# Average pooling over one axis: the last row's store moved from inside a hand-synchronised section to behind it

## The chip, the cores and the metric

One core of one Trainium2 chip. The metric is the device time of one execution in microseconds (us), median of several runs; lower is better. The profile is one execution taken by the hardware profiler; its span is about 1.8 us shorter than the timed value of the same execution (1553.8 against 1555.6 for the kernel before). Every run in this document is of the fast state, with a granted clock of 1.0; the kernel does not use the TensorE at all.

## The reference

`x` is 64 x 256 x 8192 in float32; each group of four neighbours along the last axis is averaged.

```python
def reference(x, kernel_size, stride):          # both 4
    ...
    for i in range(out_len):                    # out_len = 2048
        start = i * stride
        output[:, :, i] = np.mean(x[:, :, start : start + kernel_size], axis=2)
    return output
```

That is 536.87 MB to read, 134.22 MB to write, and three additions and one multiplication per output.

## The kernel before

The 16384 rows are cut into 64 tiles of 128 partitions x 2 rows: 8.39 MB in, 2.10 MB out each. SP (SyncE) issues the loads into two input buffers, VectorE adds pairs twice, ScalarE multiplies by 1/4 in place and issues the store. There are four output buffers. All of this stands in a critical section: a stretch in which the author places every wait by hand and the framework (the layer that otherwise places waits) puts in none. Only the end matters here. `E` is 15, so `E * U + 3` is the last tile. It is loaded, summed and stored in two single rows.

```python
        def store(eng, h, u, r0=0, r1=R, again=False):
            eng.wait_ge(s_act, h * U + (u + 1 + (r1 - 1 if r1 - r0 < R else 0)))
            eng.dma_start(
                out=og[:, h * U + u, r0 * OL : r1 * OL], in_=obuf(u, r0, r1)
            ).then_inc(s_out[u] if again else s_fin, 16)
...
        # SP's stream, behind all loads:
        for u in range(1, U - 1):
            store(nc.sync, E, u)                 # tiles 1 and 2 of the last four
        store(nc.sync, E, U - 1, R - 1, R)       # last row of the last tile
...
        # ScalarE's stream at the end:
        scale(E, 1)
        scale(E, 2)
        scale(E, 3, 0, 1)
        store(nc.scalar, E, 3, 0, 1)             # first row of the last tile
        scale(E, 3, 1, 2)

    with tc.tile_critical():                     # a second section
        nc.sync.wait_ge(s_out[0], E * 16 + 16)
        nc.sync.wait_ge(s_fin, 64)               # the four late stores have landed
```

"Ring" in this document means the queue that one issuing engine feeds: SP's is q1 in the profile, ScalarE's is q10.

Of the kernel before, what the change touches and what calls it, by code (L numbers as in the profile page):

```python
# [1 line left out]

# [4 lines left out]



_R = 2  # L10

_NIN = 2
_NOUT = 4


@with_exitstack
def kernel(
    ctx: ExitStack,
    tc: tile.TileContext,
    x: bass.AP,  # L20
    kernel_size: bass.AP,
    stride: bass.AP,
    out: bass.AP,
):
    nc = tc.nc
    K = int(kernel_size)
    assert K == int(stride) == 4
    P = nc.NUM_PARTITIONS
    dt = x.dtype
    inv_k = 1.0 / float(K)  # L30

    xf = x.flatten_outer_dims()
    of = out.flatten_outer_dims()
    rows, L = xf.shape
    OL = of.shape[1]
    R = _R
    T, OT = R * L, R * OL
    assert OL * K == L and rows % (P * R * _NOUT) == 0
    NT = rows // (P * R)

    xg = xf.rearrange("(t p r) m -> p t (r m)", p=P, r=R)
    og = of.rearrange("(t p r) m -> p t (r m)", p=P, r=R)

    pool = ctx.enter_context(tc.tile_pool(name="buf", bufs=1))
    xin = pool.tile([P, _NIN * T], dt)
    res = pool.tile([P, _NOUT * OT], dt)



    s_in = [tc.alloc_semaphore(f"s_in{b}") for b in range(_NIN)]  # L50
    s_out = [tc.alloc_semaphore(f"s_out{b}") for b in range(_NOUT)]
    s_dve = tc.alloc_semaphore("s_dve")
    s_act = tc.alloc_semaphore("s_act")
    s_half = tc.alloc_semaphore("s_half")
    s_last = tc.alloc_semaphore("s_last")
    s_fin = tc.alloc_semaphore("s_fin")

    with tc.tile_critical():  # L58



        U = _NOUT
        E = NT // U - 1

        def load(h, u, r0=0, r1=R, wait=True):
            b = u % _NIN
            if wait:
                nc.sync.wait_ge(s_dve, h * U + (u - _NIN + 1))
            nc.sync.dma_start(  # L69
                out=xin[:, b * T + r0 * L : b * T + r1 * L],  # L70
                in_=xg[:, h * U + u, r0 * L : r1 * L],
            ).then_inc(s_last if r0 > 0 else s_in[b], 16)

        def obuf(u, r0=0, r1=R):
            return res[:, u * OT + r0 * OL : u * OT + r1 * OL]

        def store(eng, h, u, r0=0, r1=R, again=False):
            eng.wait_ge(s_act, h * U + (u + 1 + (r1 - 1 if r1 - r0 < R else 0)))
            eng.dma_start(
                out=og[:, h * U + u, r0 * OL : r1 * OL], in_=obuf(u, r0, r1)  # L80
            ).then_inc(s_out[u] if again else s_fin, 16)

        def pairs(out, src):
            v = src.rearrange("p (m k) -> p m k", k=2)
            return nc.vector.tensor_tensor(  # L85
                out=out, in0=v[:, :, 0], in1=v[:, :, 1], op=mybir.AluOpType.add
            )

        def add_up(h, u, r0=0, r1=R):

            b = u % _NIN
            if r0 > 0:
                nc.vector.wait_ge(s_last, 16)
            else:
                nc.vector.wait_ge(s_out[u], h * 16)
                nc.vector.wait_ge(s_in[b], h * (U // _NIN * 16) + (u // _NIN + 1) * 16)  # L96
            src = xin[:, b * T + r0 * L : b * T + r1 * L]
            half = src[:, : (r1 - r0) * L // 2]
            pairs(half, src).then_inc(s_half, 1)
            nc.vector.wait_ge(s_half, h * U + (u + 1 + (r0 > 0)))  # L100
            pairs(obuf(u, r0, r1), half).then_inc(s_dve, 1)

        def scale(h, u, r0=0, r1=R):
            nc.scalar.wait_ge(s_dve, h * U + (u + 1 + (r0 > 0)))
            o = obuf(u, r0, r1)
            nc.scalar.mul(o, o, inv_k).then_inc(s_act, 1)  # L106



        for u in range(_NIN):  # L110
            load(0, u, wait=False)
        with nc.sync.Fori(0, E) as h:
            for u in range(_NIN, U + _NIN):
                load(h, u)
        for u in range(_NIN, U - 1):
            load(E, u)
        for r in range(R):
            load(E, U - 1, r, r + 1, wait=r == 0)
        for u in range(1, U - 1):
            store(nc.sync, E, u)  # L120
        store(nc.sync, E, U - 1, R - 1, R)


        with nc.vector.Fori(0, E) as h:
            for u in range(U):
                add_up(h, u)
        for u in range(U - 1):
            add_up(E, u)
        for r in range(R):
            add_up(E, U - 1, r, r + 1)  # L130



        scale(0, 0)
        nc.scalar.wait_ge(s_dve, 2)
        store(nc.scalar, 0, 0, again=True)
        with nc.scalar.Fori(0, E) as h:
            for u in range(1, U + 1):
                v = u % U
                nc.scalar.wait_ge(s_dve, h * U + (u + 1))  # L140
                nc.scalar.mul(obuf(v), obuf(v), inv_k).then_inc(s_act, 1)  # L141
                nc.scalar.wait_ge(s_act, h * U + (u + 1))
                nc.scalar.dma_start(out=og[:, h * U + u, :], in_=obuf(v)).then_inc(
                    s_out[v], 16
                )
        scale(E, 1)
        scale(E, 2)
        scale(E, 3, 0, 1)
        store(nc.scalar, E, 3, 0, 1)
        scale(E, 3, 1, 2)  # L150


    with tc.tile_critical():
        nc.sync.wait_ge(s_out[0], E * 16 + 16)
        nc.sync.wait_ge(s_fin, 64)


# [1 line left out]
_INS = ['x', 'kernel_size', 'stride']  # L159
_OUTS = [((64, 256, 2048), 'float32')]  # L160

_NUMBERS = {'kernel_size': 4, 'stride': 4}


# [26 lines left out]
```

## Time and profile before

| | before |
|---|---|
| time, median of 3 (range) | 1555.30 us (1555.29 to 1555.41) |
| span of the profile | 1553.8 us |
| data moved, mean rate | 671.10 MB, 432 GB/s |
| VectorE, ScalarE busy | 54%, 15% |
| one period of two tiles in mid-run | 48.36 us |

The page of the kernel before, its span, the DMA row (busy tenths in 40 equal slices) and the chain that ended last:

```profile
span 1553.8 us, 982 instructions
...
DMA  9999999999999999999999999999999999999999
...
HBM read 536.87 MB, written 134.22 MB: 432 GB/s over the span
...
DMA 72%; DVE 27%; issue 0%; SPq 0%; ACT 0%; DVEq 0%
```

The 16 DMA engines are at least nine tenths busy in every slice. The chain names VectorE (DVE) for 27%, but while it sums, stores still stand in the rings. Two tiles (20.97 MB) take 48.36 us, which is 433.6 GB/s. The Trainium skill, "DMA: Bandwidth & Descriptors", section "Specifications", gives 435 GB/s as the ceiling of the fabric; the mid-run rate of this trace agrees with that to within half a per cent. So only the first and the last few microseconds can give anything.

The timeline of the kernel before at its end (start, duration, engine, line, operation; in brackets the idle time of the engine before it and what ended it; SPq is SP's own sequence of instructions):

```profile
1537.92 4.42 DVE L85 TENSOR_TENSOR xin<-xin 128x4096 f32<-128x4096 f32 x1 [2.84 <-DMA xin<-in_x_dram]
1542.38 2.29 DVE L85 TENSOR_TENSOR res<-xin 128x2048 f32<-128x2048 f32 x1
1544.71 1.91 ACT L106 ACTIVATE res<-res 128x2048 f32<-128x2048 f32 x1 [7.68 <-DVE res L85]
1546.64 0.33 SPq L79 DMA_DIRECT2D out_dram<-res  x1
```

The last load has landed at 1537.9, the last scaling ends at 1546.62, and the last store is issued 0.02 us later. The DMA issues on the page (KB each, median us from issue to landing) and the windows at the end (the last two numbers are DMA share and GB/s; a packet counts wholly in the window in which it starts, so a share can lie above 1):

```profile
out_dram<-res SPq DMA_DIRECT2D x2, 2048.0 KB, 27.1
out_dram<-res ACTq DMA_DIRECT2D x1, 1024.0 KB, 13.0
out_dram<-res SPq DMA_DIRECT2D x1, 1024.0 KB, 5.9
```

```profile
1547.00:1549.00 2.00, 0.00 (x0) 0.00 (x0) 0.00 (x0) 1.00 0.99 422
1549.00:1551.00 2.00, 0.00 (x0) 0.00 (x0) 0.00 (x0) 1.00 0.99 418
1551.00:1553.00 2.00, 0.00 (x0) 0.00 (x0) 0.00 (x0) 1.00 0.27 115
```

The last megabyte lands 5.9 us after its issue because older stores are still ahead of it; the engines stay full until about 1551. Finally SP's own instructions behind that landing, those of the framework's end of program (L186), then those of the second section (L153); the three numbers are shortest, median and longest duration in ns, then first and last start:

```profile
L186 SPq EVENT_SEMAPHORE  x5: 17/17/5077, 1547.4 to 1553.7; - x5
L186 SPq DRAIN  x3: 7/7/7, 1553.0 to 1553.3; - x3
L186 SPq COMPARE_BRANCH  x1: 38/38/38, 1552.7 to 1552.7; - x1
```

```profile
L153 SPq NOP  x2: 13/13/13, 1547.4 to 1553.0; - x2
L153 SPq EVENT_SEMAPHORE  x1: 17/17/17, 1552.8 to 1552.8; - x1
L153 SPq DRAIN  x1: 7/7/7, 1552.9 to 1552.9; - x1
```

SP waits 5.08 us for the last landing, until about 1552.6. Then come a branch (1552.7), a semaphore (1552.8), a drain (1552.9) and a no-operation (1553.0), which leave the section, and only then the drains and barriers of the end of the program (1553.0 to 1553.8). (The wait and the branch belong to the section, though the records put them under L186.)

### The profile page before, as it was taken

How to read it: one execution, taken by the hardware profiler on the slowest of the kernel's cores; microseconds unless marked ns; L12 is line 12 of the kernel's file. 1: busy time of each engine (PE TensorE's matmuls, PEld its weight loads, DVE VectorE, ACT ScalarE, POOL GpSimd, SP SyncE). 2: the span in 40 equal slices, each digit the busy share in tenths (PEclk: the TensorE clock that was granted, in tenths of full speed). 3: DMA queues.
4: the chain of work that ended last, by engine and by line, in shares of the span. 5: the costliest groups of instructions: out<-in, count | busy, mean ns of one | idle time of the engine just before them, and what ended most of it. 6: DMA issues, size and time to landing. Idle time of an engine off the chain costs nothing.

```text
span 1553.8 us, 982 instructions
## 1 busy us (share of the span) xinstructions
DVE 839.8 (54%) x130; ACT 232.9 (15%) x66; POOL 0.2 (0%) x4
## 2 busy tenths in 40 slices
DVE  3645546456464564654646546455464554645546
ACT  1111011110111101101011010110111101111011
POOL 0000000000000000000000000000000000000000
DMA  9999999999999999999999999999999999999999
GB/s 405 423 434 439 439 439 434 417 443 427 439 439 437 434 417 434 438 439 432 442 427 426 433 434 444 439 434 423 429 435 439 439 439 434 415 436 436 439 425 405
DMA packets 18721, 671.10 MB, mean 432 GB/s; under 512 B 2081, under 2 KB 2081, under 8 KB 2081
## 3 DMA queue, kind: packets, MB, share of 16 engines
q1 hardware_dynamic: 9792, 542.12, 80.6%
q10 hardware_dynamic: 8928, 128.98, 19.4%
q14 instruction: 1, 0.00, 0.0%
HBM read 536.87 MB, written 134.22 MB: 432 GB/s over the span
## 4 chain that ended last, share of the span: by engine, by line
DMA 72%; DVE 27%; issue 0%; SPq 0%; ACT 0%; DVEq 0%
DMA xin<-in_x_dram 72%; DVE xin L85 18%; DVE res L85 9%; SPq L69 0%; ACT res L106 0%; DVEq L96 0%; SPq L186 0%; SPq L58 0%
## 5 line engine op out<-in xcount | busy, mean ns | idle before, releaser
L85 DVE TENSOR_TENSOR xin<-xin 128x8192 f32<-128x8192 f32 (+1 forms) x65 | 556.4, 8561 | 702.7 <-DMA xin<-in_x_dram 702.7
L141 ACT ACTIVATE res<-res 128x4096 f32<-128x4096 f32 x60 | 217.0, 3616 | 1226.0 <-DVE res L85 1226.0
L85 DVE TENSOR_TENSOR res<-xin 128x4096 f32<-128x4096 f32 (+1 forms) x65 | 283.3, 4359 | 2.2
L106 ACT ACTIVATE res<-res 128x4096 f32<-128x4096 f32 (+1 forms) x5 | 14.7, 2933 | 86.8 <-DVE res L85 86.8
L106 ACT ACT_TABLE_LOAD x1 | 1.3, 1283 | 0.9 <-SPq L58 0.9
L172 POOL MEMSET const-bfloat16-1.0<- 128x1 bf16 x1 | 0.1, 102 | 0.0
L172 POOL MEMSET const-uint8-127<- 128x1 uint8 x1 | 0.1, 101 | 0.0
L172 POOL MEMSET const-float32-0.0<- 128x1 f32 x1 | 0.1, 99 | 0.2 <-issue 0.2
L172 POOL MEMSET const-float32-1.0<- 128x1 f32 x1 | 0.1, 98 | 0.0
## 6 DMA issues: line engine op xcount, KB each, us to landing
out_dram<-res ACTq DMA_DIRECT2D x61, 2048.0 KB, 52.4
xin<-in_x_dram SPq DMA_DIRECT2D x2, 4096.0 KB, 29.5
out_dram<-res SPq DMA_DIRECT2D x2, 2048.0 KB, 27.1
out_dram<-res ACTq DMA_DIRECT2D x1, 1024.0 KB, 13.0
out_dram<-res SPq DMA_DIRECT2D x1, 1024.0 KB, 5.9
xin<-in_x_dram SPq DMA_DIRECT2D x63, 34.9
```

The costliest lines, as they stand in the source:

```text
L85: return nc.vector.tensor_tensor(out=out, in0=v[:, :, 0], in1=v[:, :, 1], op=mybir.AluOpType.add)
L106: nc.scalar.mul(o, o, inv_k).then_inc(s_act, 1)
L141: nc.scalar.mul(obuf(v), obuf(v), inv_k).then_inc(s_act, 1)
L172: nc = _bacc.Bacc("TRN2", target_bir_lowering=False, num_devices=1)
```

## The change

The intent: take the last store and the waits for the late stores out of the hand-synchronised sections, so that one section is left and it does not stay open for the late stores. The last store now stands behind the section, where the framework places the wait for it. That store stands in SP's ring behind the other late ones.

```diff
-        store(nc.sync, E, U - 1, R - 1, R)
+        store(nc.sync, E, U - 1, R - 1)          # now the first row, on SP
...
         scale(E, 3, 0, 1)
-        store(nc.scalar, E, 3, 0, 1)
         scale(E, 3, 1, 2)
 
-    with tc.tile_critical():
         nc.sync.wait_ge(s_out[0], E * 16 + 16)   # now the end of the first section
-        nc.sync.wait_ge(s_fin, 64)
+
+    nc.sync.dma_start(
+        out=og[:, NT - 1, (R - 1) * OL :], in_=res[:, _NOUT * OT - OL :]
+    )
```

(The semaphore `s_fin` goes, and the helper `store` loses two arguments.)

More of the change, by code (lines that the diff above doesn't have):

```diff
@@ L55 @@
     s_last = tc.alloc_semaphore("s_last")
-    s_fin = tc.alloc_semaphore("s_fin")
     with tc.tile_critical():
@@ L75, in obuf, with store @@
             return res[:, u * OT + r0 * OL : u * OT + r1 * OL]
-        def store(eng, h, u, r0=0, r1=R, again=False):
-            eng.wait_ge(s_act, h * U + (u + 1 + (r1 - 1 if r1 - r0 < R else 0)))
+        def store(eng, h, u, r1=R):
+            eng.wait_ge(s_act, h * U + (u + (1 if r1 == R else r1)))
             eng.dma_start(
-                out=og[:, h * U + u, r0 * OL : r1 * OL], in_=obuf(u, r0, r1)
-            ).then_inc(s_out[u] if again else s_fin, 16)
+                out=og[:, h * U + u, : r1 * OL], in_=obuf(u, 0, r1)
+            ).then_inc(s_out[u], 16)
         def pairs(out, src):
@@ L135 @@
         nc.scalar.wait_ge(s_dve, 2)
-        store(nc.scalar, 0, 0, again=True)
+        store(nc.scalar, 0, 0)
         with nc.scalar.Fori(0, E) as h:
```

## The prediction

> **What bounds the kernel.** The DMA engines. The profile page shows them busy 9 tenths or more in all 40 slices, moving 671.10 MB at 432 GB/s over the 1553.8 us span. VectorE is busy 54%, ScalarE 15%. The chain of waits is 72% loads landing and 27% VectorE sums, but the queues hold stores while the sums run. So only fewer bytes, or less idle time of the 16 engines at the start or end, can shorten it. The change touches only the end.
>
> **The end now**, from the timeline and the issue records:
> - last load landed about 1537.9; the last sums and the scaling end at 1546.62;
> - last-row store (1 MB) issued on SP at 1546.64, about 5.9 us to landing (1552.55);
> - the Scalar queue's store of the row before: issued 1537.05, landed about 1550.4;
> - between 1546.6 and the end 2.07 MB still move, so about 1.0 MB of older stores stand ahead of the last 1 MB. The DMA share by stretch is 0.99 from 1547 to 1551 and 0.27 from 1551 to 1553.
> - SP's wait in the second critical section is 5.08 us (1547.5 to 1552.6); branch at 1552.7, drains and barriers 1553.0 to 1553.8.
>
> So the tail is a drain of bytes.
>
> **What the change does.** Same bytes, same 16 engines.
> 1. The next-to-last row's store moves from the Scalar ring to the SP ring, behind tile 2's store. Order only: both rings feed the same engines (the Trainium skill, "DMA: Bandwidth & Descriptors", section "Issuing engines are not separate DMA queues"; this trace agrees: 434 GB/s with both rings at 1540 to 1542, 431 with SP's almost alone at 1537 to 1540). Worth 0, at most +/-0.3 us.
> 2. The last store leaves the section, so it is issued after the section's exit instead of after the scaling semaphore. Now Scalar and Vector drain at 1547.1 and 1547.2 and SP passes at 1547.4 to 1547.5. So I expect its issue at about 1547.4 to 1547.7 instead of 1546.64: +0.8 to +1.1 us. A DMA needs about 1 us from issue to first byte (the first load: issued 0.95, first packets between 1.5 and 2.5), so its bytes could start at about 1548.5. The older stores keep the engines busy until about 1549.0 (1.0 MB at 430 GB/s = 2.4 us, an estimate). So most of the delay is hidden; engines that drain early may idle some tenths: +0 to +0.6 us.
> 3. The second section goes: SP's wait chain and branch between landing (1552.55) and the drains (1553.0) is about 0.4 us. The framework's own wait for its store replaces it: -0.3 to 0 us.
> 4. The other stores land before the last one, so no longer waiting for them gains nothing.
>
> **On the critical path:** about -0.3 to +0.6 us in 1555, under 0.05%.
>
> **Prediction:** 1555.4 us, range 1554.6 to 1556.3. Chances: faster by over 2%: 0.003; within 2%: 0.994; slower by over 2%: 0.003.
>
> **What would show each step:** (1) in the windows after 1538, still 420 to 440 GB/s, and no store issue on the Scalar queue after 1483; (2) SP's last store issue at 1547.4 to 1547.7 with landing after about 5 us rather than 5.9, and DMA share about 0.95 or more from 1547 to 1551; (3) the gap from last landing to the end of the span 1.0 to 1.3 us; everything before 1530 identical within 0.1 us.
>
> **What would make it wrong:** if section exit makes SP wait for older stores to land (then the last 1 MB runs alone: about +3 us) or if a single ring drains more slowly than two.

## The result, and the profile after

| | before | after |
|---|---|---|
| time, median (range) | 1555.36 us (1555.29 to 1555.46, 4 runs) | 1554.80 us (1554.77 to 1555.00, 4 runs) |
| ratio, 95% interval | | 0.9997, 0.9979 to 1.0014 |
| span of the profile | 1553.8 us | 1553.0 us |

A ratio is the mean time of one kernel's fast runs over that of the other's of the same rounds, so it is not quite the ratio of the medians in the table. The interval contains 1. A difference of 0.56 us in 1555 is thus not settled by this ratio; what follows rests on the traces.

The timeline of the kernel after at its end, then its issues and its windows:

```profile
1537.54 4.42 DVE L85 TENSOR_TENSOR xin<-xin 128x4096 f32<-128x4096 f32 x1 [2.86 <-DMA xin<-in_x_dram]
1541.99 2.29 DVE L85 TENSOR_TENSOR res<-xin 128x2048 f32<-128x2048 f32 x1
1544.32 1.91 ACT L106 ACTIVATE res<-res 128x2048 f32<-128x2048 f32 x1 [7.70 <-DVE res L85]
1546.36 0.33 SPq L155 DMA_DIRECT2D out_dram<-res  x1
```

```profile
out_dram<-res SPq DMA_DIRECT2D x2, 2048.0 KB, 26.1
out_dram<-res SPq DMA_DIRECT2D x2, 1024.0 KB, 9.4
```

```profile
1547.00:1549.00 2.00, 0.00 (x0) 0.00 (x0) 0.00 (x0) 1.00 1.02 430
1549.00:1551.00 2.00, 0.00 (x0) 0.00 (x0) 0.00 (x0) 1.00 1.01 426
1551.00:1553.00 2.00, 0.00 (x0) 0.00 (x0) 0.00 (x0) 1.00 0.17 70
```

Two things are to be seen. The last sums already begin 0.38 us earlier than before (1537.54 against 1537.92), in a part of the program that the change does not touch. And the store is issued 0.13 us after the last scaling (1546.23) instead of 0.02 us, so leaving the section delayed it by 0.11 us only. Why so little is shown by SP's instructions of the section's exit (L57) and by what SP waited for:

```profile
L57 SPq NOP  x2: 13/13/13, 0.7 to 1546.3; - x2
L57 SPq EVENT_SEMAPHORE  x2: 17/3512/7007, 1537.2 to 1537.4; - x2
L57 SPq COMPARE_BRANCH  x1: 38/38/38, 1537.0 to 1537.0; - x1
L57 SPq DRAIN  x1: 7/7/7, 1537.3 to 1537.3; - x1
```

```profile
SPq L57 <- DVEq L57: 7.0, 1, 7.0
...
SPq L188 <- DMA out_dram<-res: 5.4, 1, 5.4
SPq L57 <- ACTq L57: 1.9, 1, 1.9
```

SP has nothing else left to do, so it runs through the branch and the drain of the exit at 1537.0 to 1537.4, more than 9 us early, and then stands waiting for VectorE (7.0 us) and ScalarE (1.9 us). Only the handover from ScalarE is left behind the last scaling. In the kernel before, the same exit (L58 there) ran only after SP had issued the last store at 1546.64:

```profile
L58 SPq EVENT_SEMAPHORE  x2: 17/22/28, 1547.0 to 1547.2; - x2
L58 SPq DRAIN  x1: 61/61/61, 1547.1 to 1547.1; - x1
L58 SPq NOP  x1: 13/13/13, 1547.3 to 1547.3; - x1
```

And at the very end of the kernel after:

```profile
L188 SPq EVENT_SEMAPHORE  x3: 17/17/17, 1552.2 to 1552.9; - x3
L188 SPq DRAIN  x3: 7/7/7, 1552.2 to 1552.5; - x3
```

The drain of the end of the program follows the landing at once (1552.2), with no branch, semaphore and no-operation of a section in between. From the landing of the last store to the first drain of the end of the program 0.49 us pass in the kernel before (1552.54 to 1553.04) and 0.07 in the kernel after (1552.14 to 1552.21); from that drain to the end of the span it is 0.77 us in both.

To put the pieces beside each other I cut each span into three. "Last sums" is the start of the last row's first addition. "Drain" runs from there to the end of the last DMA packet (start plus duration of that packet's record in the trace). "Gap" is the rest of the span, and holds the signal of the landing, a section's exit where there is one, and the end of the program. The figures are differences of readings rounded to 0.01 us and can be off by 0.01.

| profile | last sums start | drain | gap | span |
|---|---|---|---|---|
| before | 1537.92 | 14.29 | 1.59 | 1553.80 |
| after | 1537.54 | 14.25 | 1.19 | 1552.98 |

Of the 0.82 us between these two spans 0.38 lie before the last sums, 0.04 in the drain and 0.40 in the gap.

### The profile page after: what moved, and what is told of

It is laid out like the page before. It is cut to its first block, busy times and chain, and to the rows that moved or that the text cites. A ratio compares the mean times of both kernels' runs of the same rounds, so it can differ in the third digit from the quotient of the medians.

```text
span 1553.0 us, 976 instructions
## 1 busy us (share of the span) xinstructions
DVE 839.8 (54%) x130; ACT 232.9 (15%) x66; POOL 0.2 (0%) x4
## 4 chain that ended last, share of the span: by engine, by line
DMA 72%; DVE 27%; issue 0%; SPq 0%; ACT 0%; DVEq 0%
DMA xin<-in_x_dram 72%; DVE xin L85 18%; DVE res L85 9%; SPq L68 0%; ACT res L106 0%; DVEq L96 0%; SPq L188 0%; SPq L57 0%
```

## The experiments

My theory: the drain is set by the bytes and the engines are never idle in it, so a store issued a little later costs nothing (T1). The 0.40 us in the gap come from a section's exit that no longer stands behind the last landing (T2). The 0.38 us before the last sums are chance (T3). Rivals: the start belongs to the program; one ring drains differently from two; having a second section, or having the store issued by the kernel rather than the framework, is what costs; the issue of the last store is on the critical path, or does not count at all. All ten runs gave correct results. In each of them the interval of the ratio to the kernel before contains 1, so the conclusions rest on the traces; the times stand beside them, and those of the kernel before are of the same rounds.

### The two kernels again

No edit.

> The kernel before, unchanged, run as a candidate. Theory A (the start of the trace differs between two builds by chance of the run): the first sums of tile 1 start anywhere within about 42.2 to 42.5 us and the time lies within 1555.0 to 1555.5. Theory B (the start belongs to the program): they start at 42.41 again, the third tile's at 63.46, with one small packet on queue 14, and the time is 1555.3 to 1555.5. Ratio to before 1.0000 either way.

> The kernel after, unchanged. Both theories: 0.5 to 0.6 us under the kernel before (1554.8). Theory A: its start varies from run to run, and only about 0.4 us of the gain, that at the end, comes back in every run. Theory B: tile 1's sums start at 42.26 and the third tile's at 63.06 again, no packet on queue 14.

| profile | tile 0, 1, 2 sums start | last sums start | drain | gap | span | time, median (range), 5 runs |
|---|---|---|---|---|---|---|
| before | 23.02, 42.41, 63.46 | 1537.92 | 14.29 | 1.59 | 1553.80 | (above) |
| after | 22.87, 42.26, 63.06 | 1537.54 | 14.25 | 1.19 | 1552.98 | (above) |
| b_again | 22.86, 42.27, 63.51 | 1537.99 | 14.26 | 1.62 | 1553.87 | 1555.37 (1555.13 to 1555.65) |
| a_again | 23.13, 42.53, 63.49 | 1537.97 | 14.26 | 1.19 | 1553.42 | 1555.07 (1554.71 to 1555.20) |

The kernel before took 1555.39 us in the same rounds (median of 9). The start of the same program moved by 0.26 us (22.87 and 23.13 for the kernel after), and the small packet on queue 14 of the first profile did not come back in b_again. T3 holds: the start varies. The spread of the times was wider than I had written (1555.13 to 1555.65, not 1555.0 to 1555.5). With nearly the same start of the last sums (1537.99 and 1537.97), the two spans still differ by 0.45 us, nearly all of it in the gap, and that came back. The ratio of a_again is 0.9998 (0.9984 to 1.0011), the medians of these rounds differ by 0.32 us. I had written 0.5 to 0.6 us for that difference under both theories, which missed; the clause that only about 0.4 us at the end comes back in every run fits.

### One ring instead of two

```diff
+        store(nc.sync, E, U - 1, 0, 1)
         store(nc.sync, E, U - 1, R - 1, R)
...
-        store(nc.scalar, E, 3, 0, 1)
```

> Kernel before with one part of the change: the next-to-last row's store moves to the SP ring, both sections stay. My theory: order only, so 0.0 +/- 0.15 us at the end (last landing about 14.65 us after the last load's). Rival (one ring drains the late stores faster, or slower, than two): a shift of 0.3 us or more of the last landing, with the time.

Drain 14.27, gap 1.61, 1555.31 us against 1555.39 for the kernel before. The move of the store to SP's ring is worth nothing. The Trainium skill, "DMA: Bandwidth & Descriptors", section "Issuing engines are not separate DMA queues", says that transfers run on the same 16 engines whichever engine issued them; this run agrees. The expectation says 14.65 us from the last load's landing; that figure ran to the landing, the drain of the tables runs to the last packet. Taken to the landing, it is 14.63 us in this run.

### One section, with the waits at its end

```diff
-    with tc.tile_critical():
         nc.sync.wait_ge(s_out[0], E * 16 + 16)
         nc.sync.wait_ge(s_fin, 64)
```

(the two waits now stand inside the first section)

> Kernel before with its two waits moved to the end of the first section, and the second section gone. My theory: what the change gained at the end is that no section's exit stands after the last landing; here one still stands there, so the gap from the last landing to the end of the span is 1.2 us or more, as before, and the time is within 0.2 us of before. Rival (a second section as such costs time): gap 0.85 us and 0.4 us faster.

Drain 14.26, gap 1.66, 1555.43 us against 1555.39. SP's exit of the only section, in this run:

```profile
L58 SPq EVENT_SEMAPHORE  x2: 17/22/28, 1552.6 to 1552.7; - x2
L58 SPq COMPARE_BRANCH  x1: 38/38/38, 1552.4 to 1552.4; - x1
L58 SPq DRAIN  x1: 7/7/7, 1552.7 to 1552.7; - x1
L58 SPq NOP  x1: 13/13/13, 1552.8 to 1552.8; - x1
```

The last packet ended at 1551.98. The exit runs behind it, from 1552.4 to 1552.8. A second section as such is not what costs; an exit behind the last landing is. In all twelve profiles the trace says the same: from the landing to the first drain of the end of the program 0.46 to 0.54 us pass in the five that have an exit there (before, b_again, ring_only, one_section, out_only) and 0.07 in the seven that have none, and from that drain to the end of the span it is 0.77 us in every one.

### The last store outside, a section with the waits behind it

```diff
-        store(nc.sync, E, U - 1, R - 1, R)
...
+    nc.sync.dma_start(
+        out=og[:, NT - 1, (R - 1) * OL :], in_=res[:, _NOUT * OT - OL :]
+    )
     with tc.tile_critical():
         nc.sync.wait_ge(s_out[0], E * 16 + 16)
-        nc.sync.wait_ge(s_fin, 64)
+        nc.sync.wait_ge(s_fin, 48)
```

> Kernel before with the other part of the change: the last store leaves the first section and stands behind it, the row before it stays on the Scalar ring, and a second section still waits for the four stores of the first, behind the last store. My theory: the end still has a section's exit after the last bytes, so the gap from the last packet to the end of the span is about 1.6 us as in the kernel before (1.59 and 1.62), not 1.19 as after, and the time within 0.2 us of before. Rival (handing the last store to the framework is what saves): gap about 1.2 us.

Gap 1.57, drain 14.27. Here, too, an exit stands at the end, and the gap of before is back although the framework issues the last store. So handing the store over saves nothing by itself. The median, 1555.73 us against 1555.33 (ratio 1.0001, 0.9984 to 1.0017), missed what I had written; its four runs range from 1555.18 to 1556.25, and in the profiled one the surplus lies before the last sums (1538.64), from the start of the run on (tile 2's sums began at 64.17). Why this kernel's starts scatter further than the others' is open.

### The section waits for its stores

```diff
         nc.sync.wait_ge(s_out[0], E * 16 + 16)
+        nc.sync.wait_ge(s_out[1], E * 16 + 16)
+        nc.sync.wait_ge(s_out[2], E * 16 + 16)
+        nc.sync.wait_ge(s_out[3], E * 16 + 16)
```

(on top of the kernel after)

> Kernel after, but the section waits for tiles 1, 2 and the next-to-last row to land too. My theory: those land at about 1549.6, the exit then takes some 0.4 us, the last store is issued at about 1550.0 instead of 1546.36 and runs alone: the drain (last sums' start to last packet, 14.26 us in all six profiles so far) becomes 16.2 to 17.2 us and the time 2.0 to 3.0 us longer than after. Rival (the waits inside the section cost nothing, as stores land in order anyway): drain 14.3.

The last store is issued at 1550.38. Drain 16.22, gap 1.21, time 1556.99 us against 1555.33 for the kernel before. The windows of this run show the hole:

```profile
1547.00:1549.00 2.00, 0.00 (x0) 0.00 (x0) 0.00 (x0) 1.00 1.01 430
1549.00:1551.00 2.00, 0.00 (x0) 0.00 (x0) 0.00 (x0) 1.00 0.05 21
1551.00:1553.00 2.00, 0.00 (x0) 0.00 (x0) 0.00 (x0) 1.00 0.95 393
```

The DMA engines stand idle for 1.71 us: no packet is under way between 1549.49 and 1551.21. This undoes one part of the change's intent, that the section does not stay open for the late stores, and costs 1.97 us (16.22 less 14.25). It is no gain over the kernel before, whose first section did not wait for these stores either. The time is 2.19 us over the 1554.80 of the kernel after, which ran in other rounds. Counted from the last sums, the store was issued at 12.71 us instead of 8.82, so it was 3.89 us late, of which 1.92 stayed hidden. From issue to last packet it took 3.51 us.

### The last store delayed on purpose

On top of the kernel after, a useless scaling on ScalarE of an output buffer whose store has long landed:

```diff
         scale(E, 3, 1, 2)
+        nc.scalar.wait_ge(s_out[0], E * 16 + 16)
+        nc.scalar.mul(res[:, : OL // 2], res[:, : OL // 2], inv_k)   # delay_quarter
```

`delay_half` takes `OL` elements per partition, `delay_full` takes `OT` (4096).

> Kernel after with a useless scaling of 128 x 1024 elements on ScalarE before the exit, an estimated 1.05 us (1.91 us per 2048), so the last store is issued about 1.05 us later. My theory (older stores in the ring hide a late issue for about 1.4 us): drain 14.2 to 14.45 us, time as after. Rival (issue of the last store is on the critical path): drain 15.3 us, time 1 us longer.

> The same with 128 x 2048 elements, 1.91 us. My theory: backlog ends about 1.4 us after today's first possible byte, so drain 14.6 to 15.1 us, time 0.3 to 0.8 us longer than after. Rival (issue on the critical path): drain 16.2 us. Rival (no effect while any store is in flight): 14.26 us.

> Kernel after with a useless scaling of 128 x 4096 elements (3.62 us) before the exit. Model from the runs so far: the drain is the larger of 14.26 us (all bytes, engines never idle) and the issue of the last store, counted from the start of the last sums, plus 3.51 us (from the run whose section waits for stores: issue 12.71, drain 16.22). Issue here about 12.4, so drain 15.7 to 16.1 us and time 1.4 to 1.9 us over after. Rival (the hidden delay was no slack but the store's issue does not count at all): 14.26.

The useless scaling and the issue behind it, in delay_half, then in delay_full:

```profile
1546.27 1.89 ACT L151 ACTIVATE res<-res 128x2048 f32<-128x2048 f32 x1
1548.28 0.33 SPq L157 DMA_DIRECT2D out_dram<-res  x1
```

```profile
1546.17 3.60 ACT L151 ACTIVATE res<-res 128x4096 f32<-128x4096 f32 x1
1549.89 0.33 SPq L157 DMA_DIRECT2D out_dram<-res  x1
```

| profile | issue, counted from the last sums | later than after by | drain | gap | time, median |
|---|---|---|---|---|---|
| after | 8.82 | 0 | 14.25 | 1.19 | 1554.80 |
| delay_quarter | 9.76 | 0.94 | 14.26 | 1.19 | 1555.03 |
| delay_half | 10.61 | 1.79 | 14.18 | 1.29 | 1554.93 |
| delay_full | 12.32 | 3.50 | 15.83 | 1.21 | 1556.50 |
| wait_stores | 12.71 | 3.89 | 16.22 | 1.21 | 1556.99 |

The expectation for delay_half missed: I had put the slack at 1.4 us and expected 0.3 to 0.8 us of loss, and there was none (drain plus gap 15.47 against 15.44). The slack is about 1.9 us. With it, delay_full came out as written: 12.32 plus 3.51 is 15.83, which is what was measured. So T1 holds, with a limit: a late issue costs only what exceeds the slack.

### Both rows of the last tile in the one store behind the section

```diff
-        store(nc.sync, E, U - 1, R - 1)
...
-        out=og[:, NT - 1, (R - 1) * OL :], in_=res[:, _NOUT * OT - OL :]
+        out=og[:, NT - 1, :], in_=res[:, (_NOUT - 1) * OT :]
```

> Kernel after with both rows of the last tile in the one store behind the section (2 MB), none in the section. Same bytes, same exit, but 1 MB less stands in the ring when it is issued. Model: issue at 8.82 us after the start of the last sums, plus 3.51, plus 1 MB more at 430 GB/s (2.44 us, an estimate) = 14.8 us of drain, so 0.3 to 0.8 us longer than after. Rival (the engines still have enough queued): 14.26.

Drain 14.74 (expected 14.8), gap 1.23, 1555.43 us against 1555.30 for the kernel before. The store is issued no later (8.83), but 1 MB less is queued ahead of it, and the engines run dry: no packet is under way between 1546.97 and 1547.27. The windows of this run (the kernel after had a DMA share of 0.94 and 401 GB/s in the first of them):

```profile
1545.00:1547.00 2.00, 0.00 (x0) 1.30 (x1) 0.00 (x0) 1.00 0.65 279
1547.00:1548.00 1.00, 0.00 (x0) 0.00 (x0) 0.00 (x0) 1.00 1.15 492
1548.00:1549.00 1.00, 0.00 (x0) 0.00 (x0) 0.00 (x0) 1.00 0.72 295
```

The slack is made by the store ahead of the last one. The row that the change moved into SP's ring need not be in that ring, but it must be in some ring by then.

No version that beats both kernels was suggested by these runs: the drain is bound by bytes and the gap without an exit was 1.19 to 1.29 us in all seven profiles.

## Why the prediction was right or wrong

The time, 1554.80 us, lies in the predicted range of 1554.6 to 1556.3, and "within 2%" was right. The centre, 1555.4, was 0.6 us too high, and the sign of the small difference was wrong. That the time lies in the range says little: the range is wide against the terms, two of which were mis-sized. The predicted sum on the critical path, "about -0.3 to +0.6 us", does not contain the 0.40 us that the end of the trace gained, and part of the 0.56 us did not come back in the repeats.

- **"So the tail is a drain of bytes"**: right. The drain was 14.18 to 14.29 us in nine of the twelve profiles. The other three are those whose last store was issued later than the slack allows (delay_full, wait_stores) or with a shorter queue ahead of it (both_rows).
- **Step 1, one ring instead of two, "worth 0"**: right, shown by ring_only (drain 14.27). No store was issued on the Scalar queue after 1482.64, as written; the windows of the kernel after from 1537 to 1551 gave 401 to 442 GB/s, a little wider than the 420 to 440 written.
- **Step 2, "+0.8 to +1.1 us" for the issue behind the exit**: mis-sized. It was 0.11 us. I read the exit's length from the kernel before, where SP started it after its own store (1547.0); after the change SP was idle and did most of it at 1537. The hiding was right, and stronger than written: I predicted "+0 to +0.6 us" for a delay of about one microsecond, and delays of 0.94 and 1.79 us cost nothing. Of the signs named for this step, the issue at 1547.4 to 1547.7 did not come (1546.36), nor the landing about 5 us after it (5.78); the DMA share of 0.95 or more did (1.02 and 1.01). (The landing of the Scalar queue's store, "about 1550.4" in the prediction, is 1550.10 in the trace.)
- **Step 3, the second section's exit, "-0.3 to 0 us"**: the mechanism was right, the term was too small. It is 0.40 us (gap 1.59 to 1.19) in the first pair of profiles and 0.43 (1.62 to 1.19) in the second, and one_section shows that it hangs on an exit behind the last landing, not on the number of sections. I had read "about 0.4 us" from the trace and then allowed for a replacement by the framework's own wait; that replacement cost nothing visible.
- **"Everything before 1530 identical within 0.1 us"**: wrong. The two first profiles differ by 0.4 us from tile 2 on. The repeats show that the same program does this from run to run. About 0.3 to 0.4 us of the measured 0.56 (0.32 and 0.38 as difference of medians and of means in the repeats) is the change; the rest did not come back, and I put it down to chance.
- **"About +3 us" if the exit waits for stores**: the condition did not arise. Forced by wait_stores, it cost 1.97 us of drain: 3.89 us of delay less 1.92 of slack. The prediction gives no working for its 3 us, and no slack in it.
- **"The gap from the last landing to the end of the span 1.0 to 1.3 us"**: wrong by a little. The landing was at about 1552.1 and the span ended at 1553.0, so it was 0.8 us (before: 1.26), because the exit left it.

## What to carry to other kernels

When the DMA engines are the bound, ask of a late store not when it is issued, but whether enough older bytes are still queued when it is; here, with a 1 MB store ahead of it, it could come 1.9 us later without loss; without that store (both_rows, where its bytes went with the last one) the drain grew by 0.49 us, and waiting for the older stores before issuing the last lost 2 us. In this kernel a synchronised section that ended with the wait for the last transfer put its exit in series with the end of the program (0.40 us), whereas an exit that an idle engine can run through early cost 0.11 us, and that was hidden. Before explaining half a microsecond, profile the same program twice and compare the parts that the change cannot have touched.

## What the Trainium skill lacked or had wrong

- None of the pages that I read gives the cost of leaving a critical section. Here it was about 0.4 us on SP behind the last landing (0.46 to 0.54 us from the landing to the first drain of the end of the program with it, 0.07 without, in twelve profiles), and 0.11 us where SP could start it early.
- "DMA: Bandwidth & Descriptors", section "Latency and other measured facts", gives about 600 ns to the first byte for transfers issued from SP or ScalarE. With empty rings, the first data packet of the last store was recorded 0.83 us after the start of the issue instruction, in wait_stores (1550.38 to 1551.21) and in delay_full (1549.89 to 1550.72), which is 0.50 us after that instruction's end; for the first load of the program it was 1.0 us after the start (0.95 to 1.96 in the kernel before). The page and the trace may count from different points.
- The same page, section "Anatomy of one DMA — SWDGE (gpsimd) path", fits a fixed cost of about 2.0 us for another path of issue. For this path delay_full shows 3.9 us from issue to landing of 1 MB with empty rings; less 2.44 us of data at 430 GB/s (an estimate), that leaves about 1.4 us.
- No page that I read says how far the start of one program scatters: tile 0's sums began between 22.72 and 23.33 us in twelve profiles.
